# Split weights kept in DRAM for the second phase of a hybrid attention and short-convolution layer, and another order of its products

## The chip, the cores and the metric

One core of a Trainium2 chip runs the kernel. The metric is the device time of one execution in microseconds; 1531.3 us is the median of three before the change (1529.03 to 1531.97).

## What is computed

One layer over 2048 prompt rows and 32 sample rows of 1024 numbers, in fp32:

```python
z = rmsnorm(x) @ w_in                      # q | k | v | gA | B | C | u | gB | mA | mB
attn = sliding-window attention(q, k, v)   # own chunk of 64 and the two before, with sinks
y_a = (attn * silu(gate_a)) @ w_attn_out                   # 512 -> 1024: yA
y_c = (b_gate * conv3(c_gate * u) * silu(gate_c)) @ w_conv_out   # 512 -> 1024: yB
r = x + (sigmoid(merge_a) * y_a + sigmoid(merge_c) * y_c) @ w_o
out = r + sigmoid(r @ w_ple_gate) * (p @ w_ple_proj)
```

## The kernel before

**Products in three parts.** Each fp32 operand is split into a high part h (rounded to fp32r) and the rest l; a product is h·h + h·l + l·h, three matmuls. The split of a weight piece (128 x 512 numbers, 256 KB) is a cast on ACT (`eS.copy`) and a subtraction on DVE (`eV.tensor_tensor`), the two parts standing in one tile `w` of 512 KB, of which there are WB = 5. Raw pieces `wr` are loaded from `in_wu` by SP's queue into a ring of 8 tiles of 256 KB (tag `wf`).

**Phase I** (to about 850 us) computes z in two halves of the rows with Strassen-like sums of quadrants (products p = 1 to 7 of group g, steps `(h, g, p)`). A scheduler places its instructions. The first half takes the groups g one after another. On the way `quad_sums` also adds up quadrants of W_o and W_pg for phase II and keeps the sums in DRAM (`qs`). Rows in work (evictions, loads and stores of rows) use one ring of 14 buffers, `tmp`.

**Phase II** works on four blocks of rows: 0, 1, 2 of 512, 3 of 544 (the sample rows in it). Its order on every engine is written by a planner in the kernel itself: it walks through `units`, made from the list `plan`, keeps a clock of its own (`now`, `busy`, `wire`) and lets an instruction be issued when its estimate says that operands and room are there. `plan` sets the order of the products:

- yB of all blocks, p @ W_pp (`pp`) of block 2, yA of block 0, two `pp` units of block 3;
- `o` and `pg` of block 0 (products with W_o and W_pg, eight units each);
- yA of blocks 1 and 2, then `B`: W_o and W_pg for blocks 1 and 2 together, by seven big products p per quadrant row n, 28 for each weight. p = 1, 2 and 4 take raw quadrants, the others sums from `qs`. A big product is 12 matmuls of 512 columns;
- yA of block 3 (`yA3`), one unit after each of W_pg's last seven big products, and four `pp` units of block 3 around the last yA3;
- at the end `S`: W_o and W_pg for block 3 by the same scheme (names `s50`, `s58`, 12 matmuls of 272 columns each).

Attention runs between the units, tile by tile (128 rows): transposes, normalization, a rotation on POOL (`ab`, `tt`, `kr`, `qr`), transposes back into PSUM (`pqt`, `pk`), the splits `qs` (two halves) and `KL` on DVE, scores `S`, softmax, `ptl`, output `O`. Evictions `ta`, `tb`, `tk` multiply a product in PSUM by a loaded row; `ac`, `m`, `r`, `xb`, `rq` are split rows with parts `_h` (ACT) and `_l` (DVE).

The weights come in the order `worder`. `next_loads` (line 2190) issues the loads of a unit's rows at most LEAD = 2 units ahead (5 for S) and raw pieces up to RAWS = 8 ahead, and starts a split (`split_w`, line 2175) once its piece has landed, ACT is nearly free and a `w` tile will be. Each engine then works through its own list in order; an instruction whose operand is late holds all behind it.

Of the kernel before, what the change touches and what calls it, by code (L numbers as in the profile page):

```python
# [7 lines left out]
F32 = mybir.dt.float32  # L8
F32R = mybir.dt.float32r
# [4 lines left out]
P = 128  # L14
# [13 lines left out]
WB = 5  # L28
# [13 lines left out]
def tile_hybrid_stream_step(ctx: ExitStack, tc: tile.TileContext, x, xT, pT, wu, consts, rope, ckT, cv_dup,  # L42
# [282 lines left out]
    def quad(name):  # L325
        return wp.tile([P, 4, P], F32, tag="wf", name=name, bufs=8)
# [24 lines left out]
    def quad_sums(x, n):  # L351
# [7 lines left out]
        for p, o in ((7, "sc"), (5, "a21"), (6, "a11"), (3, "a12")):  # L359
            nc.gpsimd.dma_start(out=quad_sum[x, n][:, WS[p]], in_=t[o])  # L360

    def load_w(i):
# [50 lines left out]
    def prefetch(upto):  # L413
        upto = min(upto, len(worder))
        while len(made) < upto:
            i = len(made)
            while raws[0] < min(i + raws_ahead[0], len(worder)):
                raw_of[raws[0]] = load_w(raws[0])
                raws[0] += 1
            w = wp.tile([P, 2, 4, P], F32R, tag="w", name=f"w{i}")  # L420
            n = 2 if worder[i][0] == "l" and worder[i][3] == (3 if len(worder[i][1]) == 2 else 1) else 4
            split(w[:, 0, :n], w[:, 1, :n], raw_of.pop(i)[:, :n])
            made.append(w)
# [1337 lines left out]
    def run_big(u):  # L1761
# [17 lines left out]
        for k in range(4):  # L1779
            while ("XB", x, p, k) not in have or wi >= len(w_ready) or w_ready[wi] > now[0]:  # L1780
                idle()
            hi, lo = made[wi][:, 0, k], made[wi][:, 1, k]
            xh, xl = XB[x, p, k]
# [7 lines left out]
            if n == 3:  # L1791
                free("k", 2)
                free("kx", 2)
        over.add(widx.pop(wk))
        while n_done[0] in over:
            n_done[0] += 1
        go(big_done(u, ps), now[0] + SEM, BIG_NEED.get((x, p)), -1)
# [256 lines left out]
    def run_quads(u):  # L2054
# [18 lines left out]
        for k in range(4):  # L2073
            for (n, p), wk in zip(u["parts"], u["w"]):
                wi = w_of(wk, u)
                i, half = XP[p]
                while ("X", x, i, k) not in have or wi >= len(w_ready) or w_ready[wi] > now[0]:
# [3 lines left out]
                hi, lo = made[wi][:, 0, k], made[wi][:, 1, k]  # L2081
                xs = [v[:, half * m:(half + 1) * m] for v in XQ[x, k][i]]
# [6 lines left out]
                if k == 3:  # L2089
                    over.add(widx.pop(wk))  # L2090
                    while n_done[0] in over:
                        n_done[0] += 1
        for n, p in u["parts"]:
            go(quad_done(x, n, p), now[0] + SEM, None, -1)

    def unit_of(kind, b, n):
# [63 lines left out]
    widx = {}  # L2160
    n_raw, n_hi, n_made, n_done = [raws[0]], [len(made)], [len(made)], [used[0]]
    landed = {i: 3.0 for i in range(raws[0])}
    raw_free = [6.0 if i < len(made) else 1e9 for i in range(raws[0])]
    w_ready = [0.5] * len(made)
    base = used[0]

    def w_of(key, u):
# [5 lines left out]
        return widx[key]  # L2173

    def split_w(i):
        w = wp.tile([P, 2, 4, P], F32R, tag="w", name=f"w{i}")
        src = raw_of.pop(i)
        made.append(w)
        w_ready.append(1e9)
        eS.copy(out=w[:, 0], in_=src)  # L2180
        yield {}
        eV.tensor_tensor(out=w[:, 1], in0=src, in1=w[:, 0].bitcast(F32), op=sub)
        yield {}
        w_ready[i] = now[0]
        raw_free[i] = now[0]

    x_at, load_at = [0], [0]
    LEAD, AHEAD_S, RAWS = 2, 5, 8

    def next_loads():  # L2190
# [18 lines left out]

        while n_raw[0] < len(worder) and busy["Y"] < now[0] + 0.5 and (  # L2210
                n_raw[0] < RAWS or raw_free[n_raw[0] - RAWS] <= now[0]) and n_raw[0] < len(made) + RAWS:
            i = n_raw[0]
            fin[0] = 0.0
            key = worder[i]
            t = quad(f"wr{i}")
            if key[0] in "SB" and key[3] in WS:
                eY.dma_start(out=t, in_=quad_sum[key[1:3]][:, WS[key[3]]])
            else:
                uu, s = key[2:] if key[0] == "q" else (UPP + key[2] // 2, key[2] % 2) if key[0] == "pp" else {
                    1: (key[1] + key[2], 0), 2: (key[1] + key[2], 1), 4: (key[1] + key[2] + 4, 1)}[key[3]]  # L2220
                eY.dma_start(out=t, in_=wu[uu, :, 4 * s:4 * s + 4, :])
            raw_of[i] = t
            landed[i] = fin[0] + 0.5
            raw_free.append(1e9)
            n_raw[0] += 1
        i = len(made)
        if i < n_raw[0] and landed[i] <= now[0] and i < n_done[0] + WB and now[0] >= hold[0] and busy["S"] < now[0] + (
                0.3 if i > n_done[0] + 2 else 1.5):
            go(split_w(i))

    work = [0.0]
    last_use = {k: x for x, u in enumerate(units) for k in u["w"]}
    over = set()

    def run_units():
        due()
        for x, u in enumerate(units):
# [12 lines left out]
            for j, (c0, cn) in enumerate(subs):  # L2250
# [46 lines left out]
    for i, at_ in enumerate(("yB2_5", "yA0_2", f"yA3_{NA[3][2]}", f"yA3_{NA[3][4]}", f"s{UO}_2_2")):  # L2297
        begin.append((T[at_], lambda i=i: load_p(i)))
# [101 lines left out]
```

## Time and profile before

| | |
|---|---|
| median of the runs | 1531.3 us (1529.03 to 1531.97) |
| profiled execution | 1532.24 us, of which 1530.5 us span |
| PE busy | 1501.7 us, 98% |
| DVE, ACT, POOL busy | 1206.2, 836.3, 468.3 us |
| DMA | 357.94 MB, mean 234 GB/s |
| splits of weights behind 850 us | 192 on ACT and on DVE |

Read PE's idle time first: where PE is busy all the time nothing is to be had from the others. Then ask, for each stretch with idle PE, which engine or transfer ended the wait, and what that one was doing.

### The profile page before, as it was taken

The numbers are of one execution on the slowest core, as the hardware profiler recorded it, in microseconds if no ns is written. First come the engines' busy times: TensorE is split into PE (matmuls) and PEld (weight loads), VectorE is DVE, ScalarE is ACT, GpSimd is POOL, SyncE is SP. The second block draws the span as 40 slices with busy tenths as digits, with TensorE's granted clock in tenths as the row PEclk, the third lists the DMA queues.
The fourth block names the chain that finished last, engine by engine and source line by source line (L and its number), as shares of the span: only waits on it lengthen the run. The fifth ranks groups of instructions, "written<-read, shape, count | busy, mean of one in ns | idle before, by whom it ended". The sixth has DMA issues, their size and how long they took to land.

```text
span 1530.5 us, 27077 instructions
## 1 busy us (share of the span) xinstructions
PE 1501.7 (98%) x9025; PEld 1333.8 (87%) x9025; DVE 1206.2 (79%) x2208; ACT 836.3 (55%) x1966; POOL 468.3 (31%) x634
## 2 busy tenths in 40 slices
PE   9999999999999999999999999989999999999898
PEld 7878888888889999999999889978887877888898
DVE  7896887875589766898955787898967789785886
ACT  8453354344467544434554566767775475653575
POOL 2133332332212232333232245462433334112112
PEclk9999999999999999999999999999999999999999
DMA  9479886798778845343555786685678838879998
GB/s 341 154 280 342 308 293 232 276 342 279 241 266 268 307 141 196 117 132 115 184 191 185 266 302 216 217 245 188 201 193 217 220 93 205 223 209 319 289 311 253
DMA packets 207292, 357.94 MB, mean 234 GB/s; under 512 B 24624, under 2 KB 61552, under 8 KB 207152
## 3 DMA queue, kind: packets, MB, share of 16 engines
q1 hardware_dynamic: 165216, 252.40, 50.9%
q0 software_dynamic: 32288, 85.99, 19.3%
q10 hardware_dynamic: 9648, 17.83, 3.1%
q8 instruction: 71, 1.16, 0.3%
q14 instruction: 69, 0.57, 0.1%
HBM read 238.77 MB, written 117.46 MB: 233 GB/s over the span
## 4 chain that ended last, share of the span: by engine, by line
PE 41%; DVE 5%; DMA 4%; issue 2%; ACT 1%; SPq 0%; POOL 0%; DVEq 0%; ACTq 0%
PE b L135 7%; PE yB L135 6%; PE yA L135 3%; PE o L135 3%; PE pg L135 3%; PE O L135 2%; DMA pf<-in_pT 2%; PE S L135 2%; PE s58a L135 1%; PE la L722 1%; DMA wr<-in_wu 1%; PE a L589 1%; PE a L586 1%; PE a L584 1%; PE s50a L135 1%
## 5 line engine op out<-in xcount | busy, mean ns | idle before, releaser
L586 PE MATMUL a<-x_l,w 128*128 128x264 f32 (+1 forms) x744 | 228.2, 319 | 0.0
L584 PE MATMUL a<-x_h,w 128*128 128x264 f32 (+1 forms) x744 | 227.3, 320 | 0.4 <-DVE s L790 0.4
L589 PE MATMUL a<-x_h,w 128*128 128x264 f32 (+1 forms) x744 | 201.4, 320 | 0.0
L135 ACT CAST w<-wr 128x512 fp32r<-128x512 f32 x204 | 123.7, 621 | 87.2 <-PE b L135 30.9
L135 DVE TENSOR_TENSOR w<-wr,w 128x512 fp32r<-128x512 f32 x204 | 154.0, 765 | 18.3 <-ACT w L135 16.8
L206 ACT CAST w<-wr 128x512 fp32r<-128x512 f32 (+1 forms) x180 | 110.1, 618 | 105.8 <-PE c L589 30.7
L207 DVE TENSOR_TENSOR w<-wr,w 128x512 fp32r<-128x512 f32 (+1 forms) x180 | 131.0, 738 | 36.9 <-ACT w L206 35.6
L584 PEld LDWEIGHTS a<-x_h,w 128*128 128x128 f32 x744 | 139.8, 188 | 11.0 <-DVE s L790 0.6
L586 PEld LDWEIGHTS a<-x_l,w 128*128 128x128 f32 x744 | 140.1, 188 | 10.3
L135 PE MATMUL b<-xb_h,w 128*128 128x512 f32 x448 | 142.7, 395 | 1.8 <-ACT w L135 1.1
L589 PEld LDWEIGHTS a<-x_h,w 128*128 128x128 f32 x744 | 125.2, 188 | 10.8
L722 PE MATMUL la<-x_h,w 128*128 128x264 f32 x516 | 111.9, 285 | 1.7 <-ACT w L206 1.2
L584 PE MATMUL c<-x_h,w 128*128 128x512 f32 (+1 forms) x336 | 110.5, 339 | 0.0
L586 PE MATMUL c<-x_l,w 128*128 128x512 f32 (+1 forms) x336 | 110.4, 338 | 0.0
L135 PEld LDWEIGHTS b<-xb_h,w 128*128 128x128 f32 x448 | 83.4, 188 | 21.0 <-DVE w L135 1.6
L206 ACT CAST w<-a 128x512 fp32r<-128x512 f32 x82 | 49.7, 620 | 94.3 <-DVE a L342 30.9
L589 PE MATMUL c<-x_h,w 128*128 128x512 f32 (+1 forms) x336 | 99.9, 338 | 0.0
L783 DVE SCALAR_TENSOR_TENSOR u<-u,c 128x264 f32<-128x264 f32 (+1 forms) x125 | 59.4, 507 | 42.7 <-ACT u L778 28.4
L778 ACT COPY u<-a 128x264 f32<-128x264 f32 (+1 forms) x114 | 47.4, 437 | 79.7 <-PE a L589 75.5
L135 PE MATMUL yA<-ac_h,w 128*128 128x512 f32 (+1 forms) x320 | 89.0, 358 | 1.6 <-DVE ta L135 1.0
L722 PEld LDWEIGHTS la<-x_h,w 128*128 128x128 f32 x516 | 87.0, 189 | 2.4 <-ACT w L206 1.4
L135 PE MATMUL b<-xb_l,w 128*128 128x512 f32 x224 | 88.3, 394 | 0.0
(535 smaller groups left out, 4310.2 us busy)
## 6 DMA issues: line engine op xcount, KB each, us to landing
wr<-in_wu SPq DMA_DIRECT2D x213, 256.0 KB, 4.2
a<-in_wu SPq DMA_DIRECT2D x116, 256.0 KB, 5.1
wr<-ws SPq DMA_DIRECT2D x74, 256.0 KB, 3.5
wr<-qs SPq DMA_DIRECT2D x64, 256.0 KB, 4.6
ws<-a POOLq DMA_DIRECT2D x63, 256.0 KB, 3.8
qs<-a POOLq DMA_DIRECT2D x24, 256.0 KB, 5.7
tb<-z_t SPq DMA_DIRECT2D x24, 256.0 KB, 4.9
z_t<-tb SPq DMA_DIRECT2D x24, 256.0 KB, 4.3
```

The lines of the kernel that those rows point to most:

```text
L135: return f(**kw)
L206: nc.scalar.copy(out=hi, in_=src)
L207: nc.vector.tensor_tensor(out=lo, in0=src, in1=hi.bitcast(F32), op=sub)
L584: nc.tensor.matmul(out=ps[:, :cn], lhsT=w[:, 0, k], rhs=x[0][:, c0:c0 + cn], start=first and k == 0, stop=False, skip_group_check=True)
L586: nc.tensor.matmul(out=ps[:, :cn], lhsT=w[:, 0, k], rhs=x[1][:, c0:c0 + cn], start=False, stop=False, skip_group_check=True)
L589: nc.tensor.matmul(out=ps[:, :cn], lhsT=w[:, 1, k], rhs=x[0][:, c0:c0 + cn], start=False, stop=k == 3, skip_group_check=True)
L722: nc.tensor.matmul(out=ps[:, :m], lhsT=w[:, a, k], rhs=r[:, cols], start=q in "ABG" and j == 0 and e == 0, stop=j == 1 and e == 2, skip_gr ...
L778: nc.scalar.copy(out=t[:, c0:c0 + cn], in_=ps[:, :cn])
L783: nc.vector.scalar_tensor_tensor(out=t[:, c0:c0 + cn], in0=t[:, c0:c0 + cn], scalar=-1.0, in1=ps[:, :cn], op0=mul, op1=sub)
```

## The change

Each of 52 weight pieces (W_attn_out and W_conv_out 16, W_pp 4, W_o and W_pg 32 raw half columns) is loaded in phase I, split, and both parts are stored in DRAM (`stored`, tensors `wd`, 512 KB each). Phase II uses them 128 times (several pieces twice or three times): 72 times by one load of 512 KB into a `w` tile, 56 times by two loads of 256 KB, h and l apart (`wh`, `wl`), into two tiles of the ring `wf`. Their splits in phase II are gone; those of the sums from `qs` stay. Tiles are now given out by two counts of room (`w`: 5, `wf`: 8), pieces up to LOOK = 11 ahead of the one in use. The `plan` interleaves `pp` of block 2 with yB of blocks 2 and 3, puts four `pp` units of block 3 among yA of block 0 instead of at the end, and starts yA3 four big products earlier. The computation is the same.

```diff
-    plan = [("yB", b + e, n) for b in (0, 2) for n in range(8) for e in range(2)]
-    plan += [("pp", 2, n) for n in range(8)] + [("yA", 0, n) for n in range(8)] + [("pp", 3, 0), ("pp", 3, 1)]
+    plan = [("yB", e, n) for n in range(8) for e in range(2)]
+    for n in range(8):
+        plan += [("yB", 2, n), ("yB", 3, n), ("pp", 2, n)]
+    plan += [("pp", 3, 0), ("pp", 3, 1)] + [("yA", 0, n) for n in range(5)]
+    plan += [("pp", 3, 2), ("yA", 0, 5), ("pp", 3, 3), ("yA", 0, 6), ("yA", 0, 7), ("pp", 3, 4), ("pp", 3, 5)]
...
-    plan += tail[:21]
-    for e, part in enumerate(tail[21:]):
-        plan += [part, ("yA", 3, NA[3][e])]
-    plan += [("pp", 3, 2), ("pp", 3, 3), ("yA", 3, NA[3][7]), ("pp", 3, 4), ("pp", 3, 5)]
+    plan += tail[:17]
+    late = [("yA", 3, n) for n in NA[3]]
+    for e, part in enumerate(tail[17:27]):
+        plan += [part] + ([late.pop(0)] if e not in (2, 9) else [])
+    plan.append(tail[27])
...
+    stored = {(u, e): dram.tile([P, 2, 4, P], F32, tag=f"wd{u}_{e}", name=f"wd{u}_{e}")
+              for us, es in ((range(UY, UY + 8), (1, 0)), (range(UPP, UPP + 2), (0, 1)), (range(UO, UPG + 8), (0, 1)))
+              for e in es for u in us}
+    to_store = list(stored)
+
+    def store_split():
+        u, e = to_store.pop(0)
+        raw = tmp(f"wq{u}_{e}")[:, :512]
+        nc.sync.dma_start(out=raw, in_=wu[u, :, 4 * e:4 * e + 4, :].rearrange("p a b -> p (a b)"))
+        h, lo = [tmp(f"wq{x}{u}_{e}", F32R)[:, :512] for x in "hl"]
+        split(h, lo, raw)
+        for i, v in enumerate((h, lo)):
+            nc.gpsimd.dma_start(out=stored[u, e][:, i], in_=v.bitcast(F32).rearrange("p (a b) -> p a b", a=4))
...
+    store_at = {(0, g, p): 1 for g in range(9, G) for p in (6, 3) if p == 6 or g > 11}
+    store_at.update({(0, g, 5): 1 for g in range(14, G)})
+    store_at.update({(1, g, p): 1 for g in range(5, 9) for p in (6,)})
+    store_at.update({(1, g, p): 1 for g in range(16, G) for p in (1, 6, 7, 5)})
...
-    LEAD, AHEAD_S, RAWS = 2, 5, 8
+    LEAD, AHEAD_S, LOOK = 2, 5, 11
...
+            if unit_key(key):
+                where = "w" if room["w"] > len(to_split) else "wf"
+                if where == "wf" and room["wf"] < 3:
+                    break
+                src = stored[unit_key(key)]
+                tiles = w_tiles(i, where)
+                if where == "w":
+                    eY.dma_start(out=whole[i].bitcast(F32), in_=src)
+                else:
+                    for v in range(2):
+                        eY.dma_start(out=tiles[v].bitcast(F32), in_=src[:, v])
```

How the lists of two engines move. First DVE in attention, tile 1_2 (block 1, tile 2), where the halves of its split queries stand; before:

```order
L135 TENSOR_TENSOR at1_1_11759<-O_10_12103,ga1_1_11757 128x4x64
L135 TENSOR_TENSOR qs1_2_12036<-pqt1_2_12028,qs1_2_12036 64x2x256
L135 TENSOR_TENSOR w382_12124<-wr382_11405,w382_12124 128x512
L135 TENSOR_TENSOR w383_12144<-wr383_11553,w383_12144 128x512
L135 TENSOR_TENSOR qs1_2_12036<-pqt1_2_12028,qs1_2_12036 64x2x256
```

The same place with the change:

```order
L135 SCALAR_TENSOR_TENSOR tb3_7_12227<-tb3_7_12227,yB3_7_1_12359 128x272
L135 TENSOR_TENSOR KL_10523<-pk1_2_12366,KH_10522 128x2x128
L135 TENSOR_TENSOR qs1_2_12379<-pqt1_2_12369,qs1_2_12379 64x2x256 x2
L135 RECIPROCAL se_11_12397<-se_11_12397 128x4
L135 TENSOR_TENSOR at1_0_11963<-O_9_12446,ga1_0_11961 128x4x64
```

Two splits of weights stood between the halves, and nothing does now. A tile later on DVE, where qn2_0 is what POOL's rotation of the next tile waits for; before:

```order
L135 TENSOR_TENSOR qn2_0_12261<-pq2_0_12248,ss2_0_12274 128x512
L135 SCALAR_TENSOR_TENSOR ta0_5_12166<-ta0_5_12166,yA0_5_0_12285 128x512
L135 TENSOR_TENSOR KL_10069<-pk1_3_12328,KH_10068 128x2x128
L135 SCALAR_TENSOR_TENSOR ta0_6_12222<-ta0_6_12222,yA0_6_0_12347 128x512
L135 TENSOR_TENSOR qs1_3_12342<-pqt1_3_12331,qs1_3_12342 64x2x256
L135 SCALAR_TENSOR_TENSOR m0_3_l_12367<-ta0_3_12069,m0_3_h_12366 128x512
L135 TENSOR_TENSOR ta0_6_12222<-ta0_6_12222,tc0_6_12224 128x512
L135 TENSOR_TENSOR qs1_3_12342<-pqt1_3_12331,qs1_3_12342 64x2x256
```

With the change:

```order
L135 TENSOR_TENSOR qn2_0_12744<-pq2_0_12724,ss2_0_12773 128x512
L135 TENSOR_TENSOR qs1_3_12750<-pqt1_3_12735,qs1_3_12750 64x2x256
L135 SCALAR_TENSOR_TENSOR m0_2_l_12803<-ta0_2_12523,m0_2_h_12802 128x512
L135 TENSOR_TENSOR qs1_3_12750<-pqt1_3_12735,qs1_3_12750 64x2x256
L135 TENSOR_TENSOR at1_2_12492<-O_12_12840,ga1_2_12490 128x4x64
```

The halves came nearer to qn2_0, and a split of a row still stands between them. Last SP's queue among W_pg's last big products (`pp` and `ta` are row loads of the units, `wd48`, `wd61` stored pieces of W_attn_out and W_pg); before, from yA3's third load on:

```order
L135 DMA ta3_1_16519<-z_t0_1_101 128x544
L135 DMA wr490_16544<-in_wu 128x512
L135 DMA out_yT<-c11_58_0_1_15863 128x512
L135 DMA pp1_0_16559<-z_pp4_88 128x512
L135 DMA wr491_16574<-in_wu 128x512
L135 DMA out_yT<-c11_58_1_1_15890 128x512
L135 DMA ta3_5_16581<-z_t0_5_105 128x544
L135 DMA pf2_0_16586<-in_pT 128x544
L135 DMA pf2_1_16597<-in_pT 128x544
```

With the change:

```order
L135 DMA ta3_1_16801<-z_t0_1_101 128x544
L135 DMA wh484_16805<-wd61_1_192 128x512
L135 DMA wl484_16806<-wd61_1_192 128x512
L135 DMA out_yT<-tg2_1_16636 128x512
L135 DMA pp1_1_16831<-z_pp1_85 128x512
L135 DMA w485_16836<-wd48_0_159 128x1024
L135 DMA ta3_5_16851<-z_t0_5_105 128x544
```

Between the same two row loads the two weight pieces have twice the bytes, and the rows `pf` for `pp` of block 3 are gone.

More of the change, by code (lines that the diff above doesn't have):

```diff
@@ L1191, in tile_hybrid_stream_step @@
             quad_sums(*sums_at[todo[0]])
+        for _ in range(store_at.get(todo[0], 0)):
+            store_split()
         if i in after:
@@ L1779, in run_big @@
         for k in range(4):
-            while ("XB", x, p, k) not in have or wi >= len(w_ready) or w_ready[wi] > now[0]:
+            while ("XB", x, p, k) not in have or w_ready.get(wi, 1e9) > now[0]:
                 idle()
-            hi, lo = made[wi][:, 0, k], made[wi][:, 1, k]
+            hi, lo = [v[:, k] for v in W2[wi]]
             xh, xl = XB[x, p, k]
@@ L1793, in run_big @@
                 free("kx", 2)
-        over.add(widx.pop(wk))
-        while n_done[0] in over:
-            n_done[0] += 1
+        w_over(wk)
         go(big_done(u, ps), now[0] + SEM, BIG_NEED.get((x, p)), -1)
@@ L2076, in run_quads @@
                 i, half = XP[p]
-                while ("X", x, i, k) not in have or wi >= len(w_ready) or w_ready[wi] > now[0]:
+                while ("X", x, i, k) not in have or w_ready.get(wi, 1e9) > now[0]:
                     idle()
@@ L2089, in run_quads @@
                 if k == 3:
-                    over.add(widx.pop(wk))
-                    while n_done[0] in over:
-                        n_done[0] += 1
+                    w_over(wk)
         for n, p in u["parts"]:
@@ L2102, in unit_of @@
         elif kind == "pp":
-            unit(b, n, "pp", [("pp", b, n // 2)], [("p", (b - 2) * (1 + n // 2), k) for k in range(2)], [("pp", None)],
+            unit(b, n, "pp", [("pp", b, n // 2)], [("p", (b - 2) * max(1, n // 2), k) for k in range(2)], [("pp", None)],
                  done_pp)
@@ L2160, in tile_hybrid_stream_step @@
     widx = {}
[L2161 to L2165, printed above, removed]
+    W2 = {i: (made[i][:, 0], made[i][:, 1]) for i in range(used[0], len(made))}
+    w_ready = {i: 0.5 for i in W2}
+    room = {"w": WB - len(W2), "wf": 8}
+    slot = {i: "w" for i in W2}
+    n_load, to_split, landed, whole = [len(made)], [], {}, {}
     def w_of(key, u):
@@ L2173, in w_of, with w_tiles, w_over, give @@
         return widx[key]
+    def w_tiles(i, where):
+        slot[i] = where
+        if where == "w":
+            room["w"] -= 1
+            whole[i] = w = wp.tile([P, 2, 4, P], F32R, tag="w", name=f"w{i}")
+            W2[i] = w[:, 0], w[:, 1]
+        else:
+            room["wf"] -= 2
+            W2[i] = tuple(wp.tile([P, 4, P], F32R, tag="wf", name=f"w{v}{i}", bufs=8) for v in "hl")
+        return W2[i]
+    def w_over(key):
+        i = widx.pop(key)
+        where = slot.pop(i)
+        def give():
+            room[where] += 1 if where == "w" else 2
+        at(now[0] + 0.5, give, None, -4)
     def split_w(i):
-        w = wp.tile([P, 2, 4, P], F32R, tag="w", name=f"w{i}")
+        h, lo = w_tiles(i, "w")
         src = raw_of.pop(i)
-        made.append(w)
-        w_ready.append(1e9)
-        eS.copy(out=w[:, 0], in_=src)
+        eS.copy(out=h, in_=src)
         yield {}
-        eV.tensor_tensor(out=w[:, 1], in0=src, in1=w[:, 0].bitcast(F32), op=sub)
+        eV.tensor_tensor(out=lo, in0=src, in1=h.bitcast(F32), op=sub)
         yield {}
         w_ready[i] = now[0]
-        raw_free[i] = now[0]
+        room["wf"] += 1
     x_at, load_at = [0], [0]
-    LEAD, AHEAD_S, RAWS = 2, 5, 8
+    LEAD, AHEAD_S, LOOK = 2, 5, 11
     def next_loads():
@@ L2208, in next_loads @@
             load_at[0] += 1
-        while n_raw[0] < len(worder) and busy["Y"] < now[0] + 0.5 and (
-                n_raw[0] < RAWS or raw_free[n_raw[0] - RAWS] <= now[0]) and n_raw[0] < len(made) + RAWS:
-            i = n_raw[0]
+        while n_load[0] < min(len(worder), used[0] + LOOK) and busy["Y"] < now[0] + 0.5:
+            i = n_load[0]
+            key = worder[i]
             fin[0] = 0.0
-            key = worder[i]
-            t = quad(f"wr{i}")
-            if key[0] in "SB" and key[3] in WS:
-                eY.dma_start(out=t, in_=quad_sum[key[1:3]][:, WS[key[3]]])
[L2218 to L2229, printed above, removed]
+            if unit_key(key):
[4 more added lines that the diff above has]
+                tiles = w_tiles(i, where)
+                if where == "w":
+                    eY.dma_start(out=whole[i].bitcast(F32), in_=src)
+                else:
+                    for v in range(2):
+                        eY.dma_start(out=tiles[v].bitcast(F32), in_=src[:, v])
+                w_ready[i] = fin[0] + 0.5
+            else:
+                if room["wf"] < 1:
+                    break
+                room["wf"] -= 1
+                t = quad(f"wr{i}")
+                eY.dma_start(out=t, in_=quad_sum[key[1:3]][:, WS[key[3]]])
+                raw_of[i] = t
+                landed[i] = fin[0] + 0.5
+                to_split.append(i)
@@ L2231, in tile_hybrid_stream_step @@
+            n_load[0] += 1
+        if to_split and landed[to_split[0]] <= now[0] and room["w"] > 0 and now[0] >= hold[0] and busy["S"] < now[0] + (
+                0.3 if to_split[0] > used[0] + 2 else 1.5):
+            go(split_w(to_split.pop(0)))
     work = [0.0]
     last_use = {k: x for x, u in enumerate(units) for k in u["w"]}
-    over = set()
     def run_units():
@@ L2257, in run_units @@
                     wi = w_of(wk, u)
-                    while key not in have or wi >= len(w_ready) or w_ready[wi] > now[0]:
+                    while key not in have or w_ready.get(wi, 1e9) > now[0]:
                         idle()
                     k = i % 4 + (2 * (u["n"] % 2) if wk[0] == "pp" else 0)
-                    hi, lo = made[wi][:, 0, k], made[wi][:, 1, k]
+                    hi, lo = [v[:, k] for v in W2[wi]]
                     a = operand(key)
```

26 lines of the change are left out of this document (19 added, 7 removed).

## The prediction

> **What bounds the kernel now.** I read the page's first part, then the stretches of the windows view, then the waits of PE. PE is busy nearly all the time, so only its idle time can be won.
>
> ```profile
> PE 1501.7 (98%) x9025; PEld 1333.8 (87%) x9025; DVE 1206.2 (79%) x2208; ACT 836.3 (55%) x1966; POOL 468.3 (31%) x634
> 50.00:450.00 400.00, 399.91 (x1752) 324.43 (x1751) 308.66 (x510) 176.32 (x333) 109.61 (x203) 1.00 0.80 277
> 450.00:530.00 80.00, 77.76 (x627) 76.50 (x626) 69.97 (x147) 57.61 (x130) 21.64 (x34) 1.00 0.83 285
> 530.00:850.00 320.00, 319.42 (x2618) 318.96 (x2617) 245.65 (x491) 146.78 (x316) 92.66 (x132) 1.00 0.51 163
> 1000.00:1050.00 50.00, 44.21 (x243) 38.17 (x242) 45.78 (x71) 33.46 (x97) 21.40 (x22) 0.97 0.74 208
> 1145.00:1180.00 35.00, 32.13 (x167) 26.31 (x165) 26.57 (x43) 22.12 (x62) 12.96 (x13) 0.95 0.78 213
> 1240.00:1275.00 35.00, 31.77 (x150) 25.68 (x149) 32.36 (x53) 22.57 (x56) 16.49 (x18) 1.00 0.53 125
> 1374.50:1530.50 156.00, 144.58 (x1035) 137.60 (x1033) 117.65 (x229) 85.12 (x174) 29.65 (x34) 0.98 0.98 293
> ```
>
> A row is a stretch, its length, then busy us (and count) of PE, PEld, DVE, ACT and POOL, PE's clock, the DMA share and GB/s. Of 28.8 us of idle PE, 5.8 + 2.9 + 3.2 = 11.9 lie in three stretches in the middle (attention beside yA, o, pg and the big products), and 156 - 144.58 = 11.4 in the tail, some 5 of them after the last product. Phase I (to about 850) loses 2.9, apart from the start. The granted clock is 0.95 or more. In the tail the DMA share is 0.98: two resources are full there. What PE waited for behind 850 us:
>
> ```profile
> PE S L135 <- DVE qs L135: 5.5, 2, 3.8
> PE yA L135 <- DVE ac_l L135: 2.9, 1, 2.9
> PE s50b L135 <- DVE w L135: 1.8, 1, 1.8
> PE pqt L135 <- DVE at L135: 1.8, 1, 1.8
> ```
>
> DVE ends all four. Why DVE was late stands in its timeline, with POOL's beside it, and in the durations (min/median/max in ns) of qs and m_l:
>
> ```profile
> 1005.66 0.69 DVE L135 TENSOR_TENSOR qs<-pqt,qs 64x512 fp32r<-64x512 f32 x1
> 1006.37 3.79 DVE L135 TENSOR_TENSOR w<-wr,w 128x512 fp32r<-128x512 f32 x2
> 1010.19 0.69 DVE L135 TENSOR_TENSOR qs<-pqt,qs 64x512 fp32r<-64x512 f32 x1
> 1005.52 2.72 POOL L135 TENSOR_TENSOR tt<-qn,ab 128x1024 f32<-128x1024 f32 x1
> 1007.89 1.72 POOL L135 TENSOR_TENSOR kr<-tt 128x128 f32<-128x128 f32 x2
> 1027.24 4.92 DVE L135 SCALAR_TENSOR_TENSOR m_l<-ta,m_h 128x512 fp32r<-128x512 f32 x1
> L135 DVE TENSOR_TENSOR qs<-pqt,qs x32: 683/689/696, 885.9 to 1278.6; 64x512 fp32r<-64x512 f32 x32
> L135 DVE SCALAR_TENSOR_TENSOR m_l<-ta,m_h x8: 677/683/4918, 1017.7 to 1041.8; 128x512 fp32r<-128x512 f32 x8
> ```
>
> Two splits that need 0.68 us each took 3.79 while POOL worked on a tile's rotation, and the second half of qs, which PE needed, stood behind them. Where one source is in PSUM (qs) nothing was ever held; m_l, which reads SBUF alone, was held to 4.92 us.
>
> **The change, part by part.** *Splits removed.* Per split ACT and DVE lose one instruction each; 128 of them go behind 850 us, 64 (the sums, from qs) stay.
>
> ```profile
> L135 ACT CAST w<-wr x188: 601/621/650, 862.7 to 1518.3; 128x512 fp32r<-128x512 f32 x188
> L135 DVE TENSOR_TENSOR w<-wr,w x188: 654/684/2940, 863.3 to 1519.0; 128x512 fp32r<-128x512 f32 x188
> L135 DVE TENSOR_TENSOR w<-wr,w 128x512 fp32r<-128x512 f32 x65 | 55.3, 860 | 2.0 <-ACT w L135 1.2 <-DMA wr<-in_wu 0.5
> ```
>
> ACT is freed of 128 x 0.62 = 79 us, DVE of at least 128 x 0.68 = 88. From 850 to 1200 us alone (the third row) DVE loses 65 splits and 55.3 us. None of this is PE time; it counts only by shorter waits. Of the 11.9 us: the two splits between the halves of qs1_2 are gone in the new order, so the smaller of the two qs waits, 5.5 - 3.8 = 1.7, goes. The ac_l of block 2 now stand ahead of tile 3_1's rotation, so 2.9 goes. But between the halves of qs1_3 still stands an m_l, right behind qn2_0, which starts POOL: the 3.8 may come back. Of the remaining 11.9 - 4.6 = 7.3 I take half, because DVE is less loaded but the ops that can be held are not all gone. Sum -4.6 - 3.6 = **-8.2**; bounds -11.9 (all) and +4 (one more hold as long as the longest seen, on a new victim).
>
> By the Trainium skill (SBUF — State Buffer, SBUF: two separate sides) GpSimd and a VectorE op with two SBUF inputs lock one port pair, and the loser "fully blocks". By that, m0_2_l inherits the hold and its 3.8 us stays whole, which would make the term -6.3; the qs and m_l rows agree with it.
>
> *52 pieces made in phase I.* Each adds a load, a cast, a subtraction and two stores: ACT 52 x 0.62 = 32 us, DVE 52 x 0.68 = 35. Twenty-eight fall at about 230 to 450, four near 600, twenty at about 770 to 850.
>
> ```profile
> 230.00:450.00 220.00, 220.00 (x974) 179.20 (x973) 158.74 (x263) 94.63 (x174) 55.61 (x103) 1.00 0.79 275
> 770.00:850.00 80.00, 80.00 (x659) 80.00 (x658) 49.74 (x103) 43.58 (x94) 15.56 (x18) 1.00 0.60 197
> L358 DVE TENSOR_TENSOR a<-a,a x24: 673/682/689, 96.7 to 215.3; 128x512 f32<-128x512 f32 x24
> L360 POOL DMA_DIRECT2D qs<-a x24: 539/542/556, 97.7 to 216.3; - x24
> ```
>
> DVE goes from 158.74 to 178 of 220 us, and from 49.74 to 63 of 80; ACT has more room. POOL issues 104 stores of 0.54 us, with nothing behind it but other stores. The DMA gets 28 x 0.79 = 22 MB more in 220 us: 275 GB/s becomes 375, near the best slices. The cover is that PE idled 0.09 us from 50 to 450 while the sums of W_o and W_pg were made in the same way (L358, L360). What is late if the cover fails: each piece holds three of the 14 shared row buffers until its stores land, and PE's evictions take theirs from the same ring. Bounds 0 (as there) and +11 (22 MB at 275 GB/s are 80 us of transfer, 34 more than the idle 0.21 x 220 = 46, and a third of that reaches PE). I take **+2**, near the row with 0.09.
>
> *The tail.* The four p @ W_pp units go ahead of o (loads of p and stores with them), yA of block 3 starts four big products earlier, and raw quadrants come as 512 KB.
>
> ```profile
> L135 SPq DMA_DIRECT2D ta<-z_t x8: 320/323/473, 1374.5 to 1423.2; - x8
> GB/s 262 293 323 342 309 352 311 291 278 380 309 343 266 374 284 339 398 181 129 324 190 246 383 321 342 244 272 366 377 350 232 249 264 335 300 281 312 277 166 108
> DMA packets 26388, 45.63 MB, mean 293 GB/s; under 512 B 2945, under 2 KB 6529, under 8 KB 26372
> q1 hardware_dynamic: 21128, 37.18, 67.2%
> q0 software_dynamic: 5244, 8.25, 30.5%
> ```
>
> These are the first load of yA3's rows and the DMA view from there to the end (156 us). In SP's order from that load on, before has 32 raw loads of 256 KB; the change has 37 pieces of 512 KB, 7 more loads and stores of 256 KB that slid behind the mark, and 8 fewer of 272 KB: 49 x 0.262 - 8 x 0.279 = +10.6 MB. PE's part grows by four big products less four p units: 48 products of 512 columns at 400/1752 us and 48 of 272 at 320/2618 us (rows above) are 11.0 - 5.9 = 5.1, so 161 us are at hand. Plain traffic costs 0.672 x 156 / 37.18 = 2.82 us per MB, accumulation (q0) 5.77. At 2.82 the addition is 30 us on 153 busy: 183, **22 over**. At the fastest slice, 398 GB/s, 56.2 MB need 141 us, nothing is over, and the 6.4 us of idle PE that are not the end could be won: **-6**. With plain traffic at that slice's 2.5 and accumulation at its own price it is (37.18 + 10.6) x 2.5 + 47.6 = 167, **6 over**. I take +4, nearest to this last: pieces are called 11 ahead instead of 8 and need no cast, which hides a little.
>
> The Trainium skill (DMA: Bandwidth & Descriptors, Specifications) puts HBM at about 358 GB/s per core. By that figure 56.2 MB take 157 us, an estimate, and the tail would fit; the row speaks against it, with 293 GB/s at a share of 0.98.
>
> *Sum.* -8.2 + 2 + 4 = -2.2. The profiled span of 1530.5 becomes 1528.3; that execution took 1532.24 with what lies around the span, 0.9 above the median of 1531.3, so on the median the forecast is **1529** (1526 to 1533 by itself).
>
> **The rivals.** (1) *The tail keeps up.* The queues run at their fastest slice, the waits of s50b and b for splits go with the splits: -8.2 + 2 - 6 = -12.2, **1519**. For it: slices of 380 and 398 at a full share. Against it: accumulation holds the engines twice as long per MB.
>
> (2) *The DMA engines set the end, slower.* Place: from yA3's first load to the last store. Price: halfway between 6 and 22 over, 14, with -8.2 and +2: **1539**. It decides as soon as the transfers behind that load need more than 161 us; lost cover shows as late ta and pp rows, which block DVE, and as drained output behind the last product. For it: 0.98, and DVE, which works in order, already waits for rows of yA3 (the row below, over the whole run: four times, 5.9 us at most). Against: pieces have a long lead.
>
> ```profile
> DVE ta L135 <- DMA ta<-z_t: 12.6, 4, 5.9
> ```
>
> (3) *The ring of row buffers stalls phase I*: +11 instead of +2 gives **1538**. Against: the 0.09 us.
>
> **How the numbers follow.** Forecast 0.36, rival 1 0.30, rival 2 0.28, rival 3 0.06. Within 0.2% (what a measurement of this kernel can tell from no change) is 1528.2 to 1534.4. The forecast's own range puts 0.11 of its 0.36 below that and 0.25 inside: faster 0.11 + 0.30 = 0.41, same 0.25, slower 0.34. The range runs from 1517 (rival 1 and 2 us) to 1541 (rival 2 and 2 us): the tail's far end, +22, and a middle that loses nothing are left out.
>
> **What would show it.** Middle: from 1000 to 1275 no qs behind a split, PE's idle there near 4 instead of 11.9; if it stays near 12 the held op was never the splits. Phase I: the stretch 230 to 450 with PE idle under 2. Tail: from the first ta of block 3 a DMA share of 0.98 or more with about 56 MB moved; if PE idles less than 8 us there, rival 1 holds, if over 20, rival 2. The forecast is wrong as a whole if phase I is longer by over 5 us.

## The result, and the profile after

The changed kernel takes **1591.1 us** (median of four runs, 1587.13 to 1592.48) against 1531.6 for the kernel before, measured with it: ratio **1.0386**, 95% interval 1.0362 to 1.041. It is slower by 59 us, where 1529 was forecast with 1541 as the upper end. The profiled span is 1588.1 us, 57.6 more than before.

First the page of the changed kernel, its line of busy time and its DMA total:

```profile
PE 1522.0 (96%) x9025; PEld 1348.5 (85%) x9025; DVE 1138.9 (72%) x2130; ACT 793.8 (50%) x1888; POOL 519.2 (33%) x738
...
DMA packets 230876, 431.85 MB, mean 272 GB/s; under 512 B 27984, under 2 KB 64912, under 8 KB 230736
```

DVE is busy 67 us less and ACT 42; DMA moves 74 MB more than the 357.94 of before. PE has 66.1 us idle instead of 28.8, and it is also *busy* 20.3 us longer with the same 9025 matmuls, to which the last section comes back. Where the idle time lies is seen in the windows (columns as in the prediction):

```profile
230.00:450.00 220.00, 205.28 (x870) 163.45 (x869) 154.84 (x256) 94.02 (x173) 76.84 (x143) 0.98 0.93 329
450.00:530.00 80.00, 71.94 (x491) 67.42 (x492) 66.46 (x140) 54.44 (x119) 18.97 (x33) 0.94 0.84 287
850.00:1000.00 150.00, 139.91 (x863) 126.62 (x862) 96.58 (x202) 79.84 (x235) 60.90 (x74) 0.94 0.91 311
896.50:1000.00 103.50, 98.23 (x563) 85.57 (x562) 59.62 (x131) 50.96 (x176) 43.29 (x46) 0.97 0.92 314
1000.00:1350.00 350.00, 345.68 (x1937) 297.36 (x1936) 235.46 (x458) 205.31 (x635) 144.00 (x145) 1.00 0.85 256
1409.09:1588.10 179.01, 154.45 (x1031) 144.44 (x1029) 98.39 (x197) 62.91 (x129) 32.80 (x38) 0.94 1.00 311
```

Phase I idles 22.8 us in the first two rows (before: 2.2). From 850 to 1000 it is 10.1 us (before: 0.04); phase I now ends at 896.5, as the rows below show, so 4.8 of them still belong to it and 5.3 to the start of phase II. The middle idles 4.3, and the stretch from yA3's first load to the end 24.6. Two rows date the stages. The last matmul of phase I is an `lc`; the row gives its first and last start, before and then after:

```profile
L722 PE MATMUL lc<-x_h,w x240: 279/284/391, 447.6 to 855.0; 128*128 128x264 f32 x120
```

```profile
L754 PE MATMUL lc<-x_h,w x240: 278/284/588, 465.1 to 896.5; 128*128 128x264 f32 x120
```

So phase I ends 41.5 us later. From there to yA3's first load it is 1409.1 - 896.5 = 512.6 us where it was 519.5, with 5.1 us less PE work in it by the prediction's count: 1.8 gained. From that load to the end it is 179.0 where the prediction had 161 at hand: 18 lost. 41.5 - 1.8 + 18 = 57.7, which but for rounding is the whole difference of the spans.

The three largest waits of PE from 230 to 530 us, and ACT's timeline at the 3.93 us stall (start, duration, and in brackets the idle time ahead of the instruction with what ended it):

```profile
PE a L616 <- ACT u L810: 6.5, 4, 2.9
PE la L754 <- ACT x_h L206: 4.3, 1, 4.3
PE a L616 <- ACT s L810: 4.2, 2, 3.9
```

```profile
438.05 0.62 ACT L206 CAST wqh<-wq 128x512 fp32r<-128x512 f32 x1 [1.97 <-DMA wq<-in_wu]
438.58 0.59 ACT L659 ACTIVATE m<-a 128x512 f32<-128x512 f32 x1
439.06 0.61 ACT L206 CAST w<-wr 128x512 fp32r<-128x512 f32 x1
...
440.99 0.62 ACT L206 CAST wqh<-wq 128x512 fp32r<-128x512 f32 x1 [1.31 <-DMA wq<-in_wu]
441.51 0.58 ACT L810 COPY s<-a 128x512 f32<-128x512 f32 x1
```

`s<-a` is the eviction that PE waits for. All matmuls into `a` had ended by 435.4; the eviction stood behind two casts of pieces whose raw data had not landed. Over the run ACT waits 50.8 us, 27 times, for raw pieces. This gave the theories: **T1**, the bytes of the pieces fill the DMA engines; **T2a**, casts of pieces that wait for their load hold evictions in ACT's order; **T2b**, three row buffers per piece make the shared ring of 14 short; **T2c**, the added operations themselves cost.

### The profile page after: what moved, and what is told of

Read it like the earlier page. It is cut to its first block, busy times and chain, and to the rows that moved or that the text cites. A ratio compares the mean times of both kernels' runs of the same rounds, so it can differ in the third digit from the quotient of the medians.

```text
span 1588.1 us, 27298 instructions
## 1 busy us (share of the span) xinstructions
PE 1522.0 (96%) x9025; PEld 1348.5 (85%) x9025; DVE 1138.9 (72%) x2130; ACT 793.8 (50%) x1888; POOL 519.2 (33%) x738
## 4 chain that ended last, share of the span: by engine, by line
PE 64%; DMA 14%; issue 11%; POOL 4%; DVE 4%; ACT 2%; SPq 1%; POOLq 0%; ACTq 0%; DVEq 0%
PE b L135 7%; PE a L616 5%; PE a L621 5%; PE a L618 5%; PE yB L135 4%; PE la L754 4%; PE yA L135 4%; PE o L135 3%; PE c L616 2%; PE c L618 2%; PE c L621 2%; PE pp L135 2%; DMA ta<-z_t 2%; PE pg L135 2%; PE O L135 2%
## 5 line engine op out<-in xcount | busy, mean ns | idle before, releaser
L616 PE MATMUL a<-x_h,w 128*128 128x264 f32 (+1 forms) x744 | 231.6, 324 | 13.9 <-ACT u L810 6.5
L621 PE MATMUL a<-x_h,w 128*128 128x264 f32 (+1 forms) x744 | 202.7, 322 | 0.7 <-DVE w L207 0.7
L207 DVE TENSOR_TENSOR w<-wr,w 128x512 fp32r<-128x512 f32 (+1 forms) x176 | 134.9, 776 | 32.0 <-ACT w L206 32.0
L618 PEld LDWEIGHTS a<-x_l,w 128*128 128x128 f32 x744 | 141.9, 191 | 10.1
L754 PE MATMUL la<-x_h,w 128*128 128x264 f32 x516 | 116.0, 291 | 10.9 <-ACT x_h L206 4.3
L135 PE MATMUL b<-xb_h,w 128*128 128x512 f32 x352 | 112.1, 394 | 0.0
L135 PEld LDWEIGHTS b<-xb_h,w 128*128 128x128 f32 x352 | 65.8, 188 | 14.7 <-DVE rq_l L135 0.4
L378 POOL DMA_DIRECT2D wd<-wqh x52 | 28.3, 544 | 143.8 <-ACT wqh L206 115.3
L135 ACT CAST w<-wr 128x512 fp32r<-128x512 f32 x80 | 49.1, 622 | 52.3 <-DMA wr<-qs 27.9
L754 PE MATMUL la<-x_l,w 128*128 128x264 f32 x258 | 74.8, 290 | 0.4 <-DVE x_l L207 0.4
L135 POOL TENSOR_TENSOR ss<-ss,nhalf 128x10 f32<-128x10 f32 (+1 forms) x17 | 35.1, 2067 | 114.2 <-DVE ss L135 114.2
L135 DVE TENSOR_TENSOR w<-wr,w 128x512 fp32r<-128x512 f32 x80 | 56.4, 719 | 20.9 <-ACT w L135 20.4
```

What stands on the lines that cost most here:

```text
L135: return f(**kw)
L207: nc.vector.tensor_tensor(out=lo, in0=src, in1=hi.bitcast(F32), op=sub)
L378: nc.gpsimd.dma_start(out=stored[u, e][:, i], in_=v.bitcast(F32).rearrange("p (a b) -> p a b", a=4))
L616: nc.tensor.matmul(out=ps[:, :cn], lhsT=w[:, 0, k], rhs=x[0][:, c0:c0 + cn], start=first and k == 0, stop=False, skip_group_check=True)
L618: nc.tensor.matmul(out=ps[:, :cn], lhsT=w[:, 0, k], rhs=x[1][:, c0:c0 + cn], start=False, stop=False, skip_group_check=True)
L621: nc.tensor.matmul(out=ps[:, :cn], lhsT=w[:, 1, k], rhs=x[0][:, c0:c0 + cn], start=False, stop=k == 3, skip_group_check=True)
```

## The experiments

All medians in one table, each beside the kernel before as measured with it; the last column is the end of phase I from the `lc` row of each trace (before: 855.0).

| run | us | before | ratio (95%) | phase I ends |
|---|---|---|---|---|
| piecesonly | 1573.6 | 1531.1 | 1.0274 (1.0257 to 1.0291) | 898.4 |
| planonly | 1522.0 | 1531.1 | 0.9939 (0.9922 to 0.9955) | 852.4 |
| tailraw | 1576.8 | 1531.1 | 1.0295 (1.028 to 1.0311) | 898.2 |
| fourpieces | 1544.8 | 1534.0 | 1.0077 (1.005 to 1.0105) | 855.1 |
| storeraw | 1547.9 | 1534.0 | 1.01 (1.0068 to 1.0132) | 873.0 |
| nostores | 1557.1 | 1529.8 | 1.0182 (1.0156 to 1.0208) | 882.4 |
| loadahead | 1566.5 | 1534.0 | 1.0222 (1.0187 to 1.0257) | 892.5 |
| nowait | 1552.9 | 1530.7 | 1.0143 (1.0123 to 1.0163) | 879.9 |
| spread | 1580.3 | 1534.0 | 1.0305 (1.0274 to 1.0336) | 902.6 |
| spreadraw | 1536.7 | 1529.8 | 1.0045 (1.0028 to 1.0063) | 857.4 |
| spreadahead | 1567.8 | 1529.8 | 1.0252 (1.0237 to 1.0268) | 890.6 |
| spreadnowait | 1549.8 | 1530.7 | 1.0126 (1.0099 to 1.0153) | 873.8 |
| piecespool | 1675.1 | 1529.8 | 1.0949 (1.0933 to 1.0966) | 994.9 |
| tworow | 1575.2 | 1530.6 | 1.0295 (1.0278 to 1.0312) | 898.3 |
| ownring | 1575.0 | 1530.6 | 1.0291 (1.0269 to 1.0312) | 900.1 |
| spreadown | 1573.5 | 1530.6 | 1.0278 (1.0263 to 1.0293) | 895.7 |

### The parts of the change, one by one

**piecesonly**: the kernel before, with `store_split` at its 52 places (the diff's `stored`, `store_split` and `store_at`, nothing else).

> The kernel before with the 52 pieces made in phase I at the same places, and nothing reads them: phase II and its plan are untouched. Theory 1 (making them costs phase I and the start): 1531.5 + 30 + 19 = 1580 us. Theory 2 (the late start is the 512 KB loads): 1531.5 + 30 = 1561 us. If the pieces cost as the prediction had it: 1533 us.

42 us, between the two: phase I ends 43.4 us later, and all of the loss is there.

**planonly**: the kernel before, with the new `plan`, the new places of `load_p` and the two lines that go with it (the row index of `pp` and the `free("k", ...)` after it).

> The kernel before with the new plan of phase II alone (yB and pp interleaved, pp of block 3 among yA of block 0, yA of block 3 four big products earlier); all splits stay in phase II. Theory A (the middle was won by the removed splits): idle PE from 1000 to 1275 us stays at about 12 us, the tail gains a little room: 1531 us, within 3. Theory B (it was won by the new places of the rotations and ac_l): the middle loses about 4 us, 1523 to 1526 us.

Theory B, and more: 9 us faster than before. The new order alone, with every split still in phase II, beats both kernels. The same windows row, before and then with the plan alone:

```profile
1000.00:1300.00 300.00, 288.12 (x1528) 243.37 (x1527) 251.89 (x427) 194.40 (x555) 123.38 (x125) 0.99 0.70 192
```

```profile
1000.00:1300.00 300.00, 293.40 (x1584) 248.37 (x1583) 251.52 (x437) 197.37 (x570) 126.86 (x125) 1.00 0.72 199
```

Idle PE in the middle falls from 11.9 to 6.6 us, with the same load on DVE. Of the 8.3 us between the two profiled spans these are 5.3; another 2.6 lie in phase I, which ends at 852.4 instead of 855.0 although the plan is one of phase II, so they can hardly be the plan's.

**fourpieces**: the changed kernel, reading 128 times from four pieces. (A version that made none, nopieces, gave no time.)

```diff
-    to_store = list(stored)
+    to_store = list(stored)[:4]
+    made_of = {x: to_store[i % 4] for i, x in enumerate(stored)}
...
-                src = stored[unit_key(key)]
+                src = stored[made_of[unit_key(key)]]
```

> The changed kernel with only four of the 52 pieces made (the four near 600 us); phase II issues all its loads as in the changed kernel, each from one of these four, so yA, yB, pp and the raw quadrants take wrong weights and are not the reference's numbers. Alone, making the pieces cost 42 us and the plan gained 9. If the two parts add up, 1591 - 42 = 1549 us, PE idle under 4 us from 50 to 850 us, about 7 us of loss left at the start of phase II (the 512 KB loads that yB needs at once) and the tail's 29 us as it is. If the start of phase II is all due to the pieces, 1542 us; if it is all due to the loads, 1561.

11 us above the kernel before. Counted from the 1531.5 of the expectation that is 1542, the case that puts the late start of phase II on the making of the pieces. Phase I ends at 855.1 again, and of the 10.1 us of idle PE from 850 to 1000 there are 1.9:

```profile
850.00:1000.00 150.00, 148.13 (x920) 132.18 (x919) 97.36 (x213) 82.88 (x275) 61.06 (x62) 0.99 0.87 291
```

With planonly's -9.1 the reading of pieces (and the making of four) costs 10.8 + 9.1 = 20, if the parts add up, and the making of the other 48 accounts for 59.4 - 10.8 = 48.6 of the change, 6 more than alone, which the intervals of the ratios do not tell from nothing.

At the start of phase II PE's longest wait in the changed kernel is for rows of attention, `zq`. SP's timeline has five raw loads of pieces and, later, the load of these rows; the last line is the matmul that waits for it:

```profile
874.11 15.48 SPq L374 DMA_DIRECT2D wq<-in_wu  x5
...
916.55 0.37 SPq L135 DMA_DIRECT2D zq<-z_q  x1
922.67 1.09 PE L135 MATMUL pq<-cst,zq 128*128 128x128 f32 x4 [4.40 <-DMA zq<-z_q]
```

PE starts 6 us after the load is issued, in a stretch (900 to 932 us) in which the DMA engines are busy all the time and move 385 GB/s, among it loads of stored pieces. The five raw loads hold SP for 15.5 us, 13.7 of them in waits for buffers of the shared row ring. Whether that backlog made `zq` late is not shown; in fourpieces, which doesn't have it, PE waits 1.9 us for `zq`.

**tailraw**: the changed kernel, with S's raw quadrants loaded by 256 KB and split as before.

```diff
-        if key[0] in "BS" and key[3] not in WS:
+        if key[0] == "B" and key[3] not in WS:
...
```

> The changed kernel with the 24 raw pieces of S (W_o and W_pg for block 3) loaded raw by 256 KB and split in phase II as before: 6.3 MB less behind yA3. Theory 1 (the tail waits for DMA bytes): at 2.82 us per MB 17.7 us of transfer less, the stretch from 1450 us on loses 12 to 18 us of its idle PE, 1573 to 1579 us. Theory 2 (the tail's stalls are the order of the queue, or the last evictions): 1588 to 1593 us.

14 us less than the changed kernel (1576.8 against 1591.1; beside before 45.7 instead of 59.4). PE's waits in the last stretch, first of the changed kernel (from 1450 us), then of tailraw (from 1440):

```profile
PE s58a L135 <- ACT e L135: 4.9, 1, 4.9
PE s50a L135 <- ACT e L135: 3.9, 2, 2.1
PE s50a L135 <- DMA wh<-wd: 3.7, 2, 2.1
PE s50b L135 <- DMA w<-wd: 2.6, 1, 2.6
```

```profile
PE s50b L135 <- DVE w L135: 5.4, 2, 3.8
PE s58b L135 <- DVE w L135: 1.3, 1, 1.3
```

Waits for stored pieces and for the eviction `e` give way to smaller ones for splits. Theory 1 holds by the time; idle PE from 1450 us on falls from 24.5 to 15.2, by 9 us where it wanted 12 to 18.

### What in the making costs

**storeraw** (the raw piece stored twice, no split) and **nostores** (split, but not stored):

```diff
-        split(h, lo, raw)
-        for i, v in enumerate((h, lo)):
+        for i, v in enumerate((raw, raw)):
```

> The kernel before with pieces that are loaded and stored twice as they are: the same three transfers of 256 KB in the same queues, no cast on ACT, no subtraction on DVE, one row buffer instead of three. Theory T1 (DMA bytes stall phase I): 1565 to 1575 us, as with the split pieces (1573.6). Theory T2a (casts waiting for their raw piece stand in ACT's order ahead of evictions) and T2b (three row buffers held until the stores land): 1532 to 1540 us.

> The kernel before with pieces that are loaded and split at the places of the change but not stored: a third of the bytes, the same casts and subtractions in ACT's and DVE's order, row buffers free after the split. T1 (bytes): a third of the loss, 1531.5 + 42 / 3 = 1545 us or less. T2a (casts that wait for their raw piece hold evictions): loads still queue behind SP's other loads, 1552 to 1570 us.

All the bytes without the splits cost 14 us, a third of the bytes with the splits 27. T1 alone is out: it wanted 1565 or more, and 1545 or less. T2a was too strong in its first form: the transfers alone still cost 14, though no cast of a piece is there.

**spread** makes all 52 pieces at 580 to 860 us, **spreadraw** the same without splits:

```diff
+    store_at = {(1, g, p): 1 for g in range(5, 18) for p in (1, 6, 7, 5)}
```

> The kernel before with all 52 split pieces made in the second half of phase I (four per group from group 5 to 17, about 590 to 790 us), where the DMA share before is 0.5 to 0.6. T1: the 41 MB find idle transfer time, 1533 to 1540 us. T2a and T2b: a piece still puts a waiting cast ahead of evictions and holds three buffers; with loads that land in 3 us the casts wait less, 1540 to 1555 us.

> The kernel before with 52 pieces in the second half of phase I (as in the run spread: the same places, transfers and bytes), but stored twice as they are, without cast and subtraction. T1 (bytes): as with the split, 1575 to 1580 us. T2a (order on ACT): where the DMA engines have room the bytes cost nothing, 1531 to 1538 us.

spread missed every expectation: no better, rather worse (46 us). Without the split the same bytes at the same places cost 7. The waits of spread between 590 and 850 us, and SP's and ACT's timelines at one of five such stalls:

```profile
ACT wqh L206 <- DMA wq<-in_wu: 80.6, 36, 5.2
...
PE la L736 <- ACT o L792: 24.1, 5, 6.1
```

```profile
722.54 4.55 SPq L395 DMA_DIRECT2D wr<-ws  x2
727.34 6.95 SPq L370 DMA_DIRECT2D wq<-in_wu  x3
```

```profile
726.73 0.63 ACT L206 CAST w<-wr 128x512 fp32r<-128x512 f32 x1
732.53 0.62 ACT L206 CAST wqh<-wq 128x512 fp32r<-128x512 f32 x1 [5.17 <-DMA wq<-in_wu]
...
734.81 0.65 ACT L792 COPY u<-a 128x264 f32<-128x264 f32 x2
735.35 0.67 ACT L792 COPY o<-a 128x264 f32<-128x264 f32 x2
```

A load of weight sums holds SP until its buffer is free, the raw piece is issued behind it at 727.3, its cast waits on ACT to 732.5, and behind four more casts and an eviction `o` starts at 735.4; PE's wait for it ends at 735.8, after 5.6 us. The DMA share in this stretch is 0.71, so bandwidth is not what is short; PE idles 7 of 60 us:

```profile
710.00:770.00 60.00, 52.97 (x413) 52.55 (x412) 49.70 (x88) 26.01 (x52) 31.07 (x53) 0.94 0.71 238
```

**loadahead** and **spreadahead** issue each raw load two or three steps earlier:

```diff
+        if ahead_at.get(todo[0]):
+            load_piece()
...
+    ahead_at = {steps[at_step[k] - 2][0]: 1 for k in store_at}
```

> The kernel before with the 52 split pieces, but each raw piece is loaded two steps (some 7 us) before the step that splits and stores it: same bytes, same casts, row buffers held longer. Theory T2a (ACT's casts wait for raw pieces): the stalls behind u and s go, 1540 to 1555 us. Theory T1 (bytes): 1570 to 1576 us. Theory T2b (row buffers): 1574 to 1590 us, worse than with the load beside the split (1573.6).

> The kernel before with the 52 split pieces in the second half of phase I (as in the run spread), each raw piece loaded three steps ahead of the step that splits it: same bytes, same casts, row buffers held longer. T2a (casts wait for raw pieces that SP issued late): 1540 to 1560 us against 1580.3. T2b (row buffers): 1580 us or more. T1 (bytes): no change, 1577 to 1583 us.

Both gain, 10 us in place (32.5 over before instead of 42.4), 8 in spread (38.0 instead of 46.3): loadahead less than T2a wanted, spreadahead too. In spreadahead ACT's waits for raw pieces fall from 80.6 to 11.5 us, but others take their place; in place they fall from 47.9 to 14.5, and only 10 us are won. loadahead shows one that is left: its longest stall (PE 10.7 us) comes from ACT waiting for rows of the second half, again a cast whose load is late, on other data. Why those rows were late was not traced:

```profile
451.44 1.25 ACT L206 CAST x_h<-xr 128x528 fp32r<-128x528 f32 x2 [9.37 <-DMA xr<-xc]
452.61 0.58 ACT L797 COPY u<-a 128x512 f32<-128x512 f32 x1
```

**tworow** (low part over the raw piece, two buffers instead of three) and **ownring**, **spreadown** (five buffers of their own):

```diff
-        h, lo = [tmp(f"wq{x}{u}_{e}", F32R)[:, :512] for x in "hl"]
+        h, lo = tmp(f"wqh{u}_{e}", F32R)[:, :512], raw.bitcast(F32R)
```

> The kernel before with the 52 split pieces at the places of the change, but the low part is written over the raw piece: two row buffers per piece instead of three, all else the same. T2b (the shared ring): the loss falls by up to a third, 1555 to 1566 us against 1573.6. T2a (orders of ACT and SP) and T1 (bytes): 1570 to 1576 us.

> The kernel before with the 52 split pieces at the places of the change in five buffers of their own, two per piece: nothing is taken from the shared ring; orders and bytes as before. T2b: the ring's part goes, 1545 to 1558 us, and loads of rows are no longer issued in late bursts. T2a and T1: as tworow, 1566 to 1576 us (a load that waits for its own ring may hold SP and cost more).

> The kernel before with the 52 split pieces in the second half of phase I (as in the run spread, 1580.3) in five buffers of their own, two per piece. T2b: 1535 to 1555 us. T2a (casts wait in ACT's order for raw pieces that SP issued late): 1565 to 1585 us.

tworow changes nothing (44.6 over before), against T2b. The other two are void for that question: once they had their own buffers, the scheduler put the pieces elsewhere, loads and casts at 27 to 424 us in both. Row of ownring:

```profile
L370 SPq DMA_DIRECT2D wq<-in_wu x52: 327/402/1659, 27.0 to 411.9; - x52
```

They only add a third place at which the pieces cost the same, 43 to 44 us.

**nowait** and **spreadnowait** keep bytes, places and operations and take the same buffers (two of the three come free earlier, behind the subtraction instead of behind the stores); the cast and subtraction read a tile that is always there, and the raw piece is stored twice:

```diff
-        split(h, lo, raw)
-        for i, v in enumerate((h, lo)):
+        split(h, lo, pcs)
+        for i, v in enumerate((raw, raw)):
```

> The kernel before with pieces at the places of the change whose raw part is loaded and stored twice as it is, while the cast and the subtraction at the same places work on a tile that is always there (their results are read by nobody): same bytes, same three row buffers, same operations, but no cast waits for its raw piece. T2a (the waiting cast holds evictions): as with raw pieces and no casts, 1546 to 1553 us. If the operations themselves cost (T2c, busy time of ACT and DVE): 1566 to 1576 us, near the 1573.6 of the split pieces.

> The same in the second half of phase I, against the run spread (1580.3, with waits) and spreadraw (1536.7, no operations). T2a: 1535 to 1545 us. T2c: 1570 to 1582 us.

The wait is worth 42.4 - 22.2 = 20 us in place and 46.3 - 19.2 = 27 in spread. T2a is the largest part, but not alone; spreadnowait is above its range for T2a. That two buffers come free earlier does not explain the gain: SP's waits at its loads of pieces, which need nothing but a free row buffer, do not move with the loss. They are 26.0 us in piecesonly, 36.6 in nowait and 26.2 in storeraw (42, 22 and 14 us lost), and 51.4 in spread, 51.3 in spreadnowait and 46.0 in spreadraw (46, 19 and 7 lost).

**piecespool** puts all of a piece's work on POOL:

```diff
-        nc.sync.dma_start(out=raw, ...
+        nc.gpsimd.dma_start(out=raw, ...
-        split(h, lo, raw)
+        nc.gpsimd.tensor_copy(out=h, in_=raw)
+        nc.gpsimd.tensor_tensor(out=lo, in0=raw, in1=h.bitcast(F32), op=sub)
```

> The kernel before with the 52 split pieces at the places of the change, but all of a piece's work on POOL (its load issued there, cast, subtraction, stores): same bytes, same three row buffers, held longer; nothing in the orders of SP, ACT and DVE. T2a (order on ACT and SP): what is left is what the bytes cost, as with raw pieces stored twice (1547.9): 1543 to 1555 us. T2b (three row buffers held): 1573 us or more. T1: 1570 to 1576 us.

A plain miss, 145 us over before. The wait moved to the engine that also stores rows; the group of casts and one of the waits that follow from it (230 to 600 us):

```profile
L372 POOL CAST wqh<-wq 128x512 fp32r<-128x512 f32 x52 | 36.0, 692 | 128.4 <-DMA wq<-in_wu 72.9 <-issue 28.5 <-ACT ycs_h L210 5.2
```

```profile
DVE xq L509 <- DMA xq<-xc: 49.3, 5, 14.5
```

POOL stood 128 us ahead of these casts, the stores of rows (`xc`) queued behind, DVE waited up to 14.5 us for rows read back, and PE for DVE. It is the same mechanism on a worse engine, and no test of T2b.

## Why the prediction was wrong, step by step

**Phase I, +2: this step failed** (41.5 us; alone 43.4). The prediction took its value from the row with 0.09 us of idle PE, "while the sums of W_o and W_pg were made in the same way". They were not made the same way where it counts: a sum is four loads, four additions on DVE and four stores, with nothing on ACT; a piece puts a cast on ACT, whose order also holds the evictions that PE waits for. The prediction counted ACT's time (32 us, and room for it) and not its order. What stands behind an instruction it asked of POOL alone ("with nothing behind it but other stores"). The parts as measured, by difference to before: transfers 13.9 us (storeraw), the operations 8.3 more (nowait), their wait for the raw piece 20.2 more (piecesonly). In spread the three are 6.9, 12.3 and 27.1. By the intervals of the ratios each difference of two runs is known to some 3 to 6 us, so the 8.3 is the least certain. What within the 13.9 is bandwidth and what SP's order was not taken apart; at 590 to 850 us, with room on the DMA engines, 6.9 stay. The upper bound of +11 counted bytes alone, so it missed the larger part.

**Rival 3** had phase I as the loser, with the ring of row buffers as the cause: 0.06 and +11. The place was right. As the main cause the ring is not supported: two buffers instead of three changed nothing (tworow), and SP's waits for a row buffer are as long where 7 us are lost as where 46 are. That the ring is short is true all the same: those waits are 31.4 us in the changed kernel, 13.7 of them at the five loads from 874 us on. What they cost by themselves was not measured; an untouched ring at the same places was not reached.

**The middle, -8.2: right in size, in part by luck.** Idle PE falls from 11.9 us to 4.3, the "near 4" that was to show it. What the order does (-4.6 in the prediction) is 11.9 - 6.6 = 5.3 by planonly, and the rest, put at -3.6, is 6.6 - 4.3 = 2.3. The `ac_l` wait of 2.9 is gone, as forecast. But in planonly the waits for `qs` fall from 5.5 to 0.2, more than the 1.7 of the sum, and new ones take their place: 2.6 for `pp` on ACT, and 3.1 instead of 1.0 for `ptl`. So the halves agree as sums, not wait by wait. The hold that "may come back" between the halves of qs1_3 did, in DVE's timeline of the changed kernel, with POOL's beside it:

```profile
1073.67 0.68 DVE L135 TENSOR_TENSOR qs<-pqt,qs 64x512 fp32r<-64x512 f32 x1
1074.39 2.70 DVE L135 SCALAR_TENSOR_TENSOR m_l<-ta,m_h 128x512 fp32r<-128x512 f32 x1
1077.10 0.69 DVE L135 TENSOR_TENSOR qs<-pqt,qs 64x512 fp32r<-64x512 f32 x1
1073.50 3.04 POOL L135 TENSOR_TENSOR tt<-qn,ab 128x256 f32<-128x256 f32 x2
```

PE waits 2.7 us for that second half. By the Trainium skill (SBUF — State Buffer, SBUF: two separate sides), m0_2_l had to inherit the hold; the trace agrees, with 2.70 us while POOL works on `tt`.

**The start of phase II was not in the sum.** PE waits 5.3 us there (`zq` 4.4, a stored piece `w` 0.9), and its clock is 0.97 in the row from 896.5 us on (before: 1.00 from 850 to 1000). Together with the middle, 1.8 us are left of the gain.

**The tail, +4: right mechanism, mis-sized** (18). The transfer was counted well: 55.69 MB from yA3's first load on, where 56.2 were forecast, at a share of 1.00; 24.6 us of idle PE, over the 20 that were to show rival 2. The sum had three prices and chose the fastest slice, 2.5 us per MB. In the changed kernel plain traffic costs

```profile
q1 hardware_dynamic: 23904, 46.84, 71.9%
q0 software_dynamic: 5474, 8.69, 27.5%
```

0.719 x 179 / 46.84 = 2.75 us per MB and accumulation 5.7: the measured means, by which the prediction had +22. A mean over 156 us at a share of 0.98 was already the speed to count on; taking one slice of 40 as a lasting rate was the fault. The 18 us show as 13 more of idle PE (24.6 instead of 11.4) and 5 of longer busy time. By the Trainium skill's figure (DMA: Bandwidth & Descriptors, Specifications) the tail would have fitted in an estimated 157 us; at 311 GB/s it did not.

## What to carry to other kernels

Before work is put on an engine with idle time, ask what it waits for and what stands behind it in that engine's order: here casts of 0.62 us held PE for up to 6.1 us (spread), because they waited for loads that another engine's queue had issued late. Work that was covered elsewhere is no proof of cover unless it used the same engines. Where a change mixes a new order with new data, time the order alone: it gave 0.9939 here, and the whole change 1.0386.

## What the runs showed of the hardware

A stall costs more than its idle time. After the 3.93 us stall of the changed kernel, PE's timeline:

```profile
437.59 0.39 PE L618 MATMUL c<-x_l,w 128*128 128x512 f32 x1
437.81 0.40 PE L621 MATMUL c<-x_h,w 128*128 128x512 f32 x1
442.14 0.79 PE L616 MATMUL a<-x_h,w 128*128 128x512 f32 x1 [3.93 <-ACT s L810]
442.73 0.63 PE L618 MATMUL a<-x_l,w 128*128 128x512 f32 x1
443.16 0.63 PE L621 MATMUL a<-x_h,w 128*128 128x512 f32 x1
```

Matmuls of 512 columns start 0.22 to 0.24 us apart ahead of it and 0.43 behind it, for ten in a row: 2 us on top of 3.93. Over the run PE is busy 20.3 us longer with the same 9025 matmuls, a third of the loss, which no count of idle time shows. The granted clock fits that: its mean over the span is 0.980 instead of 0.995, which makes an estimated 1588.1 x 0.020 - 1530.5 x 0.005 = 24 us of lost clock, a part of it while PE stood. The stall and the clock behind it agree with the Trainium skill (TensorE: Matmul & The Clock Gate, Part 1), by which an idle window of some 3.4 us halves the clock until PE has been busy as long again.
